# A list scheduler for one in-order TensorE stream: PSUM banks by readiness, small products collected, traced latencies, and an even spread of large products

## The chip, the cores and the metric

The kernel runs on one core of one Trainium2 chip. The metric is the device time of one execution in microseconds (us); of several executions the median is given. TensorE (PE in the profile) multiplies matrices into PSUM, which has eight banks here, each one 128 x 512 fp32 tile. VectorE (DVE) and ScalarE (ACT) do elementwise work, GpSimd (POOL) a few memsets, SyncE (SP) issues the DMAs. Each engine runs its own instructions in the order in which the program issues them.

## The reference

Two layers of a streaming encoder over x of 512 tokens x 1024 channels, all in fp32. Cut to what matters:

```python
for l in range(DEPTH):                                        # DEPTH = 2
    x = x + 0.5 * swiglu_ffn(rmsnorm(x, ffn1_norm[l]), ffn1_w_in[l], ffn1_w_out[l])
    h = rmsnorm(x, mix_norm[l])
    u_rwkv, u_gla, u_xa, u_gate = split_cols(h @ w_in[l], ...)
    y_rwkv, v_first = rwkv7_mixer(u_rwkv, v_first, ...)       # 8 heads of 64, a recurrence over the tokens
    y_gla = gla_mixer(u_gla, ...)                             # 4 heads, chunked linear attention, chunks of 64
    y_xa = memory_attention(u_xa, rmsnorm(mem, mem_norm[l]), xa_w_kv[l])   # 4 heads over 256 memory rows
    gates = jax.nn.sigmoid(u_gate.reshape(b, s, 3, d))
    merged = jnp.einsum('bsjc,jcd,bsjd->bsd', branches, w_branch[l], gates)
    x = x + merged @ w_out[l]
    x = x + 0.5 * swiglu_ffn(rmsnorm(x, ffn2_norm[l]), ffn2_w_in[l], ffn2_w_out[l])
return rmsnorm(x, final_norm)
```

The RWKV recurrence is, per token, `state = state * w + (state . -kk)(kk * a) + v k` and `y = state . r`.

## The kernel before

**Two kinds of products.** A large product is a projection of 128 output channels over all 512 tokens. Its operands are split into a high and a low part (`split` and `weight`: ScalarE writes the high part `whi`, VectorE subtracts it for the low part `wlo`), and for each 128 input channels three passes run (`mm3`: high x high, high x low, low x high), so that a projection of 1024 channels is 24 passes into one PSUM bank, `ps_b`. Small products are those inside RWKV, GLA and the attention heads and in the norms: fp32 matmuls of 64 to 512 columns, each of which runs as two passes, and transposes. They go into the banks `ps_i`, `ps_f`, `ps_c` and `ps_y`.

**PSUM.** Three banks have the tag b (large products), two the tag i (RWKV `gates` and `first`, GLA), and one each f (RWKV `second` and `out`, attention heads, norms, GLA), c (RWKV `inverse`, GLA) and y (RWKV `second`, GLA, and in layer 1 the value product of `rwkv_lora`). A tag is a ring: in the kernel before, the n-th tile of a tag waits, in program order, until the tile that used the same bank last is gone.

**RWKV in units.** Four pairs of heads (`hp`) times two halves of 256 tokens (`hf`) make eight units in a layer. `rwkv_rkv(hp)` multiplies the large products for k and r of a pair into `rk_k` and `rk_r`, each a single buffer. For a unit `rwkv_gates`, `rwkv_first` and `rwkv_inverse` prepare four chunks of 64 tokens (inverse: X, W and Z go round between VectorE and TensorE), `rwkv_second` runs the recurrence over them (per chunk the products S,AR into y, then qs,Z and VU,KBT into f, each waiting for VectorE or ScalarE), its last products are VU,GR, and `rwkv_out` normalises y with a row of small VectorE operations, transposes it (`ps_f<-cst,y`) and multiplies the output gate (`ps_f<-sgl,g`). In `rwkv_fill` the preparation of unit n is recorded ahead of `second` and `out` of unit n-1.

**Fills.** Between the units `rwkv_fill` records independent work with many large products, 18 fills: an attention head (a query projection of 24 passes and its small products), four parts of the GLA branch, a second head, four more parts of the GLA branch, and eight parts of the attention branch. A part of a branch is a gate projection of 24 passes and a branch projection of 12. `share` says how many fills are recorded after each unit; the k and r of the next pair come after them. After the eight units six gates of the RWKV branch (`early`) are recorded. Then the RWKV branch follows: it reads the units' y back, splits it into `yh`, `yl` and multiplies it.

**The planner.** The kernel is recorded first and issued afterwards. Every engine instruction becomes an `Op` with its dependencies; `cost` gives it two prices: `busy`, for which it holds its engine, and `took`, after which its result is there. `lag` adds what lies between two operations: `HOP` (34 ns), and ahead of a TensorE operation 120 ns and a margin, `SLACK`, or 400 ns behind a DMA. `run` simulates all engines; where TensorE is free it takes, in the kernel before, the ready operation with the smallest key `(kind, n)`: small products (kind 0) always ahead of large ones (kind 1), and within a kind by program order n. VectorE and ScalarE take what is due first (`late`, which `urgency` works out from TensorE's order in the pass before). `plan` makes six such passes and keeps the order that ends first by its own clock; `issue` then emits the instructions in that order. Durations of the plan do not reach the chip, only the order does: TensorE waits in its queue for each product's operands. Because all instructions are issued from one place, the profile shows one line, L278, for all of them; they are told apart by their tiles.

Of the kernel before, what the change touches and what calls it, by code (L numbers as in the profile page):

```python
# [11 lines left out]
F32 = mybir.dt.float32  # L12
# [7 lines left out]
P = 128  # L20
T = 512
# [60 lines left out]
class Tile:  # L82
    def __init__(self, pool, shape, dt, name, tag, bufs):
        self.pool, self.shape, self.dt, self.name, self.tag, self.bufs = pool, shape, dt, name, tag, bufs
        self.real, self.users, self.writes, self.reads, self.runs = None, [], [], [], ([], [])
        self.before, self.gone = (), None

# [105 lines left out]
class Pool:  # L193
# [6 lines left out]

    def tile(self, shape, dt, name, tag, bufs=None):
# [30 lines left out]
class Op:  # L232
    def __init__(self, n, engine, what, call, deps):
        self.n, self.engine, self.what, self.call = n, engine, what, call
        self.deps, self.kind, self.pool, self.tile = deps, 1, None, None
        self.busy = self.took = self.start = 0.0
        self.mode = self.table = None

# [9 lines left out]
class Recorder:  # L248
# [3 lines left out]
    def __init__(self, tc):  # L252
        self.tc, self.ops, self.open, self.closed, self.entered, self.kind = tc, [], [], [], [], 0
        for e in self.ENGINES:
            setattr(self, e, Engine(self, e))
# [14 lines left out]
    def add(self, engine, what, a, k):  # L270
# [9 lines left out]
        o = self.op(engine, what, call, ())  # L280
        deps = o.deps
        for v, writes in [(v, False) for v in ins] + [(v, True) for v in outs]:
            t, area = v.tile, v.area()
            assert t.gone is None
            if not t.users or writes:
# [69 lines left out]

    HOP, SLACK = 34, 150

    def lag(self, p, o, slack=True):
# [8 lines left out]
        return self.HOP + s + (120 if o.engine == "tensor" else 0)  # L367

    def run(self, late):

# [5 lines left out]
        events, count, table, last, done = [], 0, None, None, 0  # L376
        order = []
# [22 lines left out]
        while events:  # L400
            t, _, what, o = heapq.heappop(events)
            touched = set()
            while True:
                if what == "ready":
                    if o.engine is None:
                        o.start = t
                        order.append(o)
                        free_up(o)
                    else:
                        heapq.heappush(ready[o.engine], (*key(o), o))  # L410
                        touched.add(o.engine)
                else:
                    touched.add(o)
                if events and events[0][0] <= t:
                    t, _, what, o = heapq.heappop(events)
                else:
                    break
            for e in touched:
                if free[e] > t or not ready[e]:
                    continue  # L420
                if e == "scalar":
                    best = min(ready[e], key=lambda q: q[0] + (2000 if q[-1].table not in (None, table) else 0))
                    ready[e].remove(best)
                    heapq.heapify(ready[e])
                    o = best[-1]
                else:
                    o = heapq.heappop(ready[e])[-1]
                o.start = t
                busy = o.busy
                if e == "tensor":  # L430
                    if last is not None and o.mode != last:
                        busy += 28 if o.mode[1:] == last[1:] else 92
                    last = o.mode
                if e == "scalar" and o.table is not None and o.table != table:
                    table = o.table
                    o.start += 1290
                    busy += 1290
# [24 lines left out]

    def plan(self, passes=6):
        for o in self.ops:
            o.next = []
# [29 lines left out]
class Net:  # L495
# [232 lines left out]
    def rwkv_lora(self):  # L728
        nc = self.nc
        self.wlal = self.lr.tile([P, T], F32, name="wlal", tag="wlal", bufs=1)  # L730
        self.shifted(12, self.wlal)
        nc.scalar.activation(self.wlal[0:64, :], self.wlal[0:64, :], AF.Tanh)
        if self.l > 0:
            ps = self.psy.tile([P, T], F32, name="ps_y", tag="y")
        for q in range(4):
# [12 lines left out]
    def rwkv_rkv(self, hp):  # L748
        nc = self.nc
        wz = self.const.tile([P, 2, P], F32, name="wz", tag="wz", bufs=2)  # L750
        nc.sync.dma_start(out=wz, in_=self.I["wz"][self.l, hp])
# [22 lines left out]
    def rwkv_gates(self, hp, hf, wz, r, k, v):  # L774
        nc, t1 = self.nc, self.t256
        N = 256
        cs = slice(hf * N, (hf + 1) * N)
# [30 lines left out]
    def rwkv_first(self, hp, hf, r, k, v, kk, kh, a, G):  # L808
        nc, rw, t1 = self.nc, self.rw, self.t256
        N = 256  # L810
        ch = lambda a: a.rearrange("p (c t) -> p c t", c=4)
# [97 lines left out]
    def rwkv_inverse(self, Z, AB, AU, W32):  # L909
        nc, rw = self.nc, self.rw  # L910
        flat = lambda q: q.rearrange("p u t -> p (u t)")

# [39 lines left out]
    def rwkv_second(self, hp, hf, E, AR, VU, u0, GR, Z, KBT, bv):  # L952
        nc, rw, t1 = self.nc, self.rw, self.t256
        N = 256
        cs = slice(hf * N, (hf + 1) * N)
        y = t1("y", 2)
        for c in range(4):
# [30 lines left out]

        psy = self.psy.tile([P, T], F32, name="ps_y", tag="y")
        for p in range(2):  # L990
# [10 lines left out]
    def rwkv_out(self, hp, hf, y, bv):  # L1001

        nc, rw, t1 = self.nc, self.rw, self.t256
        N = 256
        cs = slice(hf * N, (hf + 1) * N)
# [90 lines left out]
    def xa_head(self, pool, j, q, kT, vm):  # L1096
        nc = self.nc
        sc = 128.0 ** -0.5
        for hh in range(2):
# [27 lines left out]
    def gla_conv(self, pool, i, out):  # L1127
        nc = self.nc
        ps = self.proj(GQKV + i)
        a = pool.tile([P, T], F32, name="gc", tag="gc", bufs=2)  # L1130
# [6 lines left out]
    def gla_al(self, pool):  # L1137
        nc = self.nc
        w = self.weight(self.I["w_al"][self.l], KD, 16)
        ps = self.big()  # L1140
# [6 lines left out]
    def gla_decay(self, pool, hp, al):  # L1147
        nc = self.nc
        ps = self.small()
        nc.tensor.matmul(ps, self.aup[:, hp * P:(hp + 1) * P], al, start=True, stop=True)  # L1150
# [13 lines left out]
    def gla_pair(self, pool, hp, al, yh, yl, between):  # L1164
        nc = self.nc
        t = lambda name, bufs=1: pool.tile([P, T], F32, name=name, tag=name, bufs=bufs)
        E, F = self.gla_decay(pool, hp, al)
        between()
        q, k = t("gq"), t("gk", 2)
        self.gla_conv(pool, hp, q)  # L1170
# [62 lines left out]
        for j in range(2):  # L1233
            h = 2 * hp + j
            ps = self.psy.tile([P, T], F32, name="ps_y", tag="y")
            for p in range(4):
# [210 lines left out]
```

## Time and profile before

| what | value |
|---|---|
| median of 3 runs | 2769.85 us (2769.09 to 2770.24) |
| the profiled execution: its time, its span | 2769.8 us, 2768.0 us |
| mean granted TensorE clock | 0.995 |
| TensorE busy | 2731.8 us (99%), 13280 matmul passes |
| VectorE, ScalarE busy | 1570.7 us (57%), 1164.9 us (42%) |
| DMA | 258.04 MB, 93 GB/s on average |

In time order, layer 0's RWKV units run from about 560 to 940 us, layer 1's from about 1925 to 2315. How to read the rows: a row of the timeline has start, duration, engine, line, operation, tile written<-tiles read, shapes, number of instructions, and in brackets the idle time of the engine ahead of it and what ended it. Matmuls are pipelined and their ends are modelled, so the step from one start to the next says more than a duration. A row of a stretch has the stretch, its length, then for TensorE, its weight loads, VectorE, ScalarE (and POOL) busy time and count, and at the end the granted clock, the share of the DMA engines and GB/s. A row for one tile has the operation, count, durations in ns (least, median, greatest) and the first and the last start.

### The profile page before, as it was taken

The page shows a single profiled execution, that of the slowest core. Times are in us where ns is not written, and L with a number is a line of the kernel's source. Part 1 is how long each engine was busy: PE and PEld are TensorE (multiplying, and loading weights), DVE is VectorE, ACT ScalarE, POOL GpSimd, SP SyncE. Part 2 cuts the span into 40 slices and gives each one's busy share as a digit, 9 for nine tenths or more (in the row PEclk, how much of TensorE's full clock was granted, in tenths as well). Part 3 has the DMA queues.
Part 4 walks back from the last instruction along what each step waited for, and adds up shares of the span by engine and source line. Part 5 has one row for each costly group of instructions (what it writes and reads, how often), then busy time and mean ns, then how long its engine had stood idle before and what let it go on. Part 6 is the DMA issues. An engine that isn't in the chain of part 4 may idle for free. (4 is left out here: it accounts for less than half of the span.)

```text
span 2768.0 us, 35481 instructions
## 1 busy us (share of the span) xinstructions
PE 2731.8 (99%) x13280; PEld 2225.2 (80%) x13280; DVE 1570.7 (57%) x3056; ACT 1164.9 (42%) x2150; POOL 19.8 (1%) x102
## 2 busy tenths in 40 slices
PE   8999999999999999999999999999999999999998
PEld 7888888887787788888888888877777877888886
DVE  6434456677668654444454343666775786543444
ACT  6323356455445343233343232664553453432332
POOL 0000000000000000000000000000000000000000
PEclk9999999999999999999999999999999999999999
DMA  5232332211222232222332323322212112322322
GB/s 194 90 101 99 102 135 77 100 59 67 85 71 68 69 115 99 89 102 94 104 107 89 102 99 114 132 83 77 67 63 91 67 58 78 117 95 89 106 90 86
DMA packets 91723, 258.04 MB, mean 93 GB/s; under 512 B 10464, under 2 KB 24832, under 8 KB 91552
## 3 DMA queue, kind: packets, MB, share of 16 engines
q1 hardware_dynamic: 91552, 255.79, 27.5%
q8 instruction: 104, 1.70, 0.3%
q14 instruction: 67, 0.55, 0.1%
HBM read 243.69 MB, written 12.06 MB: 92 GB/s over the span
## 5 line engine op out<-in xcount | busy, mean ns | idle before, releaser
L278 ACT ACTIVATE whi<-wraw 128x512 fp32r<-128x512 f32 (+1 forms) x874 | 544.0, 623 | 1191.6 <-PE ps_b L278 1155.9
L278 PE MATMUL ps_b<-xhi,whi 128*128 128x512 f32 x2288 | 905.5, 396 | 8.2 <-ACT whi L278 8.2
L278 DVE TENSOR_TENSOR wlo<-wraw,whi 128x512 fp32r<-128x512 f32 (+1 forms) x874 | 590.9, 677 | 564.3 <-ACT whi L278 549.1
L278 PE MATMUL ps_b<-xhi,wlo 128*128 128x512 f32 x2288 | 904.4, 395 | 0.0
L278 PE MATMUL ps_b<-xlo,whi 128*128 128x512 f32 x2288 | 904.3, 395 | 0.0
L278 PEld LDWEIGHTS ps_b<-xhi,whi 128*128 128x128 f32 x2288 | 429.2, 188 | 97.4 <-ACT whi L278 8.6
L278 PEld LDWEIGHTS ps_b<-xlo,whi 128*128 128x128 f32 x2288 | 429.0, 187 | 90.6 <-issue 3.5
L278 PEld LDWEIGHTS ps_b<-xhi,wlo 128*128 128x128 f32 x2288 | 429.0, 188 | 89.3 <-issue 2.5
L278 PE MATMUL ps_b<-mhi,whi 128*128 128x512 f32 x704 | 277.4, 394 | 0.0
L278 PE MATMUL ps_b<-mhi,wlo 128*128 128x512 f32 x704 | 276.0, 392 | 0.0
L278 PE MATMUL ps_b<-mlo,whi 128*128 128x512 f32 x704 | 273.2, 388 | 0.0
L278 PEld LDWEIGHTS ps_b<-mhi,wlo 128*128 128x128 f32 x704 | 132.2, 188 | 31.0
L278 PEld LDWEIGHTS ps_b<-mlo,whi 128*128 128x128 f32 x704 | 132.1, 188 | 29.6
L278 PEld LDWEIGHTS ps_b<-mhi,whi 128*128 128x128 f32 x704 | 132.4, 188 | 26.3
L278 DVE TENSOR_TENSOR fm<-ps_b,ft 128x512 f32<-128x512 f32 x88 | 60.9, 692 | 124.5 <-PE ps_b L278 124.4
L278 DVE TENSOR_TENSOR ft<-ps_b,rs 128x512 f32<-128x512 f32 x88 | 60.9, 692 | 121.5 <-PE ps_b L278 121.2
L278 PE MATMUL ps_b<-yh,whi 128*128 128x512 f32 (+1 forms) x256 | 97.2, 383 | 5.0 <-ACT yh L278 5.0
L278 ACT ACT_TABLE_LOAD x73 | 93.7, 1283 | 11.0 <-DMA par<-in_par_dram 5.6
L278 PE MATMUL ps_b<-yl,whi 128*128 128x512 f32 (+1 forms) x256 | 97.8, 382 | 0.0
L278 PE MATMUL ps_b<-yh,wlo 128*128 128x512 f32 (+1 forms) x256 | 95.8, 377 | 0.0
L278 DVE SCALAR_TENSOR_TENSOR x<-ps_b,x 128x512 f32<-128x512 f32 x64 | 44.3, 692 | 62.2 <-PE ps_b L278 62.2
L278 DVE TENSOR_TENSOR ft<-ft,rs 128x512 f32<-128x512 f32 x88 | 60.9, 693 | 14.1 <-ACT ft L278 6.3
(260 smaller groups left out, 2746.6 us busy)
## 6 DMA issues: line engine op xcount, KB each, us to landing
wraw<-in_ffn_in_dram SPq DMA_DIRECT2D x176, 512.0 KB, 3.5
wraw<-in_w_main_dram SPq DMA_DIRECT2D x108, 512.0 KB, 3.5
wraw<-in_ffn_out_dram SPq DMA_DIRECT2D x64, 512.0 KB, 3.5
wraw<-in_ffn_out_dram SPq DMA_DIRECT2D x64, 192.0 KB, 2.3
wraw<-in_w_branch_dram SPq DMA_DIRECT2D x48, 256.0 KB, 2.6
wraw<-in_w_out_dram SPq DMA_DIRECT2D x16, 512.0 KB, 3.5
xd<-x SPq DMA_DIRECT2D x16, 256.0 KB, 2.2
wraw<-in_w_k_dram SPq DMA_DIRECT2D x8, 512.0 KB, 3.6
```

The costliest lines, as they stand in the source:

```text
L278: return getattr(getattr(self.tc.nc, engine), what)(*(f(v) for v in a), **{n: f(v) for n, v in k.items()})
```

## The change

It edits the planner and the order of recording; no operation's shape, operand or number changes.

1. `cost`: the time until a TensorE result can be read is raised, for transposes from 60 to 275 ns, for large passes from n/2.4 - 36 to n/2.4 + 177, for small fp32 products from `2 passes - 45` (up to 128 columns; + 55, + 100 above) to one pass + two column times + 168. The margin `SLACK` ahead of TensorE goes from 150 to 60 ns, the price of a turn between large and small from 28 to 45, that of an activation table from 1290 to 1400.
2. `choose` replaces "small ahead of large": behind a small product, ready small products go on, those of the same shape of array first; behind a large product small ones are taken only when ready ones of 400 ns are together or one has been ready for 600 ns; otherwise the next large one goes.
3. Tiles of the tags f, c and y are made with `free=True`. They no longer wait for the tile ahead of them in program order across all parts, only for their own part's (`nc.part`: lora, rkv, gates, first, inverse, second, out, xa, gla). In `run` the first operation of such a tile takes a bank if one is free (`slot`), or is held until one is given back.
4. `rwkv_fill`: `share` goes from five fills after a unit (15 after the first three units, the rest after the fourth) to two after each of the eight, the last two behind all units.

```diff
 class Pool:
+    def tile(self, shape, dt, name, tag, bufs=None, free=False):
         t = Tile(self, shape, dt, name, tag, bufs)
+        t.free = free
         ring = self.tags.setdefault(tag, [])
-        t.before = [self.rec.gone(ring[-bufs])] if len(ring) >= bufs else list(self.before)
+        t.before = [self.rec.gone(ring[-bufs])] if len(ring) >= bufs and not free else list(self.before)
+        if free:
+            own = self.tags.setdefault((tag, self.rec.part), [])
+            if len(own) >= bufs:
+                t.before.append(self.rec.gone(own[-bufs]))
+            own.append(t)
...
     def cost(self, o, ins, outs, a, k):
             if o.what == "transpose":
-                o.busy, o.took = 109, 60
+                o.busy, o.took = 109, 275
             elif ins[0].dt == F32R:
                 o.busy = n / 2.4 + 13.7
-                o.took = o.busy - 50
+                o.took = n / 2.4 + 177
             else:
                 o.busy = 2 * max(108 if wide else 58, 2 * n / 2.4 + 2.7)
-                o.took = o.busy + (-45 if n <= 128 else 55 if n <= 256 else 100)
+                o.took = o.busy / 2 + 2 * n / 2.4 + 168
...
-    HOP, SLACK = 34, 150
+    HOP, SLACK = 34, 60
...
+    HOLD = 600
+    def choose(self, ready, last, est, t):
+        small = [q for q in ready if q[0] == 0]
+        big = min((q for q in ready if q[0]), default=None)
+        if not small:
+            return big
+        same = [q for q in small if q[-1].mode == last]
+        if same:
+            return min(same)
+        if big is None or (last is not None and not last[0]):
+            return min(small)
+        first = min(small)
+        if sum(q[-1].busy for q in small) >= 400 or t - min(est[q[-1]] for q in small) >= self.HOLD:
+            return first
+        return big
...
     def run(self, late):
+        def slot(o):
+            t = o.takes
+            if t is None:
+                return True
+            k = t.pool, t.tag
+            if used.get(k, 0) < t.bufs:
+                used[k] = used.get(k, 0) + 1
+                return True
+            held.setdefault(k, []).append(o)
+            return False
...
+                while ready[e]:
+                    if e == "tensor":
+                        o = self.choose(ready[e], last, est, t)
+                        ...
+                    if slot(o):
+                        break
...
-                        busy += 28 if o.mode[1:] == last[1:] else 92
+                        busy += 45 if o.mode[1:] == last[1:] else 92
...
     def small(self, tag="f"):
-        return self.pss.tile([P, T], F32, name="ps_" + tag, tag=tag, bufs=2 if tag == "i" else 1)
+        return self.pss.tile([P, T], F32, name="ps_" + tag, tag=tag, bufs=2 if tag == "i" else 1, free=tag != "i")
...
-                psq = self.psy.tile([P, T], F32, name="ps_y", tag="y")
+                psq = self.psy.tile([P, T], F32, name="ps_y", tag="y", free=True)
...
     def rwkv_fill(self, rkv, fill):
-        share = [0, 5, 5, 5, 5, 5, 5, 4, 4]
+        share = [0, 2, 2, 2, 2, 2, 2, 2, 2]
```

More of the change, by code (lines that the diff above doesn't have):

```diff
@@ L85, in __init__ @@
         self.real, self.users, self.writes, self.reads, self.runs = None, [], [], [], ([], [])
-        self.before, self.gone = (), None
+        self.before, self.gone, self.free = (), None, False
     def make(self):
@@ L199, in __init__ @@
             ctx.callback(self.close)
-    def tile(self, shape, dt, name, tag, bufs=None):
+    def tile(self, shape, dt, name, tag, bufs=None, free=False):
         bufs = bufs or self.bufs
         t = Tile(self, shape, dt, name, tag, bufs)
+        t.free = free
         ring = self.tags.setdefault(tag, [])
-        t.before = [self.rec.gone(ring[-bufs])] if len(ring) >= bufs else list(self.before)
+        t.before = [self.rec.gone(ring[-bufs])] if len(ring) >= bufs and not free else list(self.before)
[4 more added lines that the diff above has]
+            own.append(t)
         ring.append(t)
@@ L236, in __init__ @@
         self.busy = self.took = self.start = 0.0
-        self.mode = self.table = None
+        self.mode = self.table = self.takes = None
 class Engine:
@@ L253, in __init__ @@
         self.tc, self.ops, self.open, self.closed, self.entered, self.kind = tc, [], [], [], [], 0
+        self.part = None
         for e in self.ENGINES:
@@ L283, in add @@
             t, area = v.tile, v.area()
+            if t.free and not t.users:
+                o.takes = t
             assert t.gone is None
@@ L376, in run @@
         events, count, table, last, done = [], 0, None, None, 0
-        order = []
+        order, used, held = [], {}, {}
         def key(o):
             return (o.kind, o.n) if o.engine == "tensor" else (late[o], o.n)
+        def slot(o):
[8 more added lines that the diff above has]
+            return False
         def put(t, what, o):
@@ L408, in run @@
                         free_up(o)
+                        if o.tile is not None and o.tile.free:
+                            k = o.tile.pool, o.tile.tag
+                            used[k] -= 1
+                            for q in held.pop(k, ()):
+                                put(t + self.lag(o, q), "ready", q)
                     else:
@@ L418, in run @@
             for e in touched:
-                if free[e] > t or not ready[e]:
+                if free[e] > t:
                     continue
[L421 to L425, printed above, removed]
+                while ready[e]:
+                    if e == "tensor":
+                        o = self.choose(ready[e], last, est, t)
+                        ready[e].remove(o)
+                        heapq.heapify(ready[e])
+                        o = o[-1]
+                    elif e == "scalar":
+                        best = min(ready[e], key=lambda q: q[0] + (2000 if q[-1].table not in (None, table) else 0))
+                        ready[e].remove(best)
+                        heapq.heapify(ready[e])
+                        o = best[-1]
+                    else:
+                        o = heapq.heappop(ready[e])[-1]
+                    if slot(o):
+                        break
                 else:
-                    o = heapq.heappop(ready[e])[-1]
+                    continue
                 o.start = t
@@ L435, in run @@
                     table = o.table
-                    o.start += 1290
-                    busy += 1290
+                    o.start += 1400
+                    busy += 1400
                 free[e] = t + busy
@@ L463, in plan @@
     def plan(self, passes=6):
+        for t in {o.takes: None for o in self.ops if o.takes is not None}:
+            self.gone(t)
         for o in self.ops:
@@ L729, in rwkv_lora @@
         nc = self.nc
+        nc.part = "lora"
         self.wlal = self.lr.tile([P, T], F32, name="wlal", tag="wlal", bufs=1)
@@ L733, in rwkv_lora @@
         if self.l > 0:
-            ps = self.psy.tile([P, T], F32, name="ps_y", tag="y")
+            ps = self.psy.tile([P, T], F32, name="ps_y", tag="y", free=True)
         for q in range(4):
@@ L749, in rwkv_rkv @@
         nc = self.nc
+        nc.part = "rkv"
         wz = self.const.tile([P, 2, P], F32, name="wz", tag="wz", bufs=2)
@@ L775, in rwkv_gates @@
         nc, t1 = self.nc, self.t256
+        nc.part = "gates"
         N = 256
@@ L809, in rwkv_first @@
         nc, rw, t1 = self.nc, self.rw, self.t256
+        nc.part = "first"
         N = 256
@@ L910, in rwkv_inverse @@
         nc, rw = self.nc, self.rw
+        nc.part = "inverse"
         flat = lambda q: q.rearrange("p u t -> p (u t)")
@@ L953, in rwkv_second @@
         nc, rw, t1 = self.nc, self.rw, self.t256
+        nc.part = "second"
         N = 256
@@ L986, in rwkv_second @@
                                                        ALU.mult, ALU.add)
-        psy = self.psy.tile([P, T], F32, name="ps_y", tag="y")
+        psy = self.psy.tile([P, T], F32, name="ps_y", tag="y", free=True)
         for p in range(2):
@@ L1003, in rwkv_out @@
         nc, rw, t1 = self.nc, self.rw, self.t256
+        nc.part = "out"
         N = 256
@@ L1097, in xa_head @@
         nc = self.nc
+        nc.part = "xa"
         sc = 128.0 ** -0.5
@@ L1128, in gla_conv @@
         nc = self.nc
+        nc.part = "gla"
         ps = self.proj(GQKV + i)
@@ L1138, in gla_al @@
         nc = self.nc
+        nc.part = "gla"
         w = self.weight(self.I["w_al"][self.l], KD, 16)
@@ L1148, in gla_decay @@
         nc = self.nc
+        nc.part = "gla"
         ps = self.small()
@@ L1165, in gla_pair @@
         nc = self.nc
+        nc.part = "gla"
         t = lambda name, bufs=1: pool.tile([P, T], F32, name=name, tag=name, bufs=bufs)
@@ L1168, in gla_pair @@
         between()
+        nc.part = "gla"
         q, k = t("gq"), t("gk", 2)
@@ L1234, in gla_pair @@
             h = 2 * hp + j
-            ps = self.psy.tile([P, T], F32, name="ps_y", tag="y")
+            ps = self.psy.tile([P, T], F32, name="ps_y", tag="y", free=True)
             for p in range(4):
```

## The prediction

> **What bounds the kernel now.** I read the page's totals first, then TensorE's work by stretches, then its instructions in order of time, and last its waits.
>
> ```profile
> span 2768.0 us, 35481 instructions
> PE 2731.8 (99%) x13280; PEld 2225.2 (80%) x13280; DVE 1570.7 (57%) x3056; ACT 1164.9 (42%) x2150; POOL 19.8 (1%) x102
> ```
> TensorE is never idle for long, VectorE and ScalarE are at about a half: the end is set by TensorE's in-order stream. But "99% busy" is a modelled end, so I go by start-to-start steps. Timeline of TensorE, layer 0:
>
> ```profile
> 719.70 0.39 PE L278 MATMUL ps_b<-yh,whi 128*128 128x512 f32 x1
> 719.93 0.39 PE L278 MATMUL ps_b<-yl,whi 128*128 128x512 f32 x1
> 720.15 0.39 PE L278 MATMUL ps_b<-yh,wlo 128*128 128x512 f32 x1
> ...
> 700.74 1.00 PE L278 MATMUL ps_c<-X,abd 128*128 128x64 f32 x8
> 701.58 0.44 PE L278 MATMUL ps_y<-S,AR 128*128 128x128 f32 x2
> 701.78 0.48 PE L278 MATMUL ps_b<-xhi,whi 128*128 128x512 f32 x1
> 702.09 0.40 PE L278 MATMUL ps_b<-xlo,whi 128*128 128x512 f32 x1
> ```
> A large product (into ps_b, 512 wide) costs 0.227 us, start to start. The ten small passes and one large from 700.74 to 702.09 take 1.35 us, so a small pass takes (1.35 - 0.227) / 10 = 0.112 us, and here turning from large to small and back costs nothing. Now the count of everything, by stretch and tile (columns: stretch, TensorE busy and instructions, then weight loads, VectorE, ScalarE):
>
> ```profile
> 0.00:2768.00 2768.00, 2422.99 (x10224) 1888.37 (x10224) 269.81 (x388) 71.41 (x114) 1.00 0.28 93
> ...
> L278 PE MATMUL ps_b<-yl,whi 128*128 128x256 f32 x64 | 18.1, 283 | 0.0
> ...
> PE ps_b L278 <- ACT whi L278: 8.2, 1, 8.2
> ...
> 2757.35 2.08 PE L278 MATMUL ps_f<-cst,rt 128*128 128x128 f32 x8 [0.57 <-DVE rt L278]
> ```
> Of 10,224 passes into ps_b, 192 are 256 wide (three groups of 64; 0.120 us each), 10,032 are 512 wide: 2277.3 + 23.0 = 2300 us. The other 13,280 - 10,224 = 3,056 are small: about 2,360 at 0.112, 384 of half the columns at 0.058, 256 of 256 elements at 0.216, 56 of 512 at 0.431: 366 us. The first weights come at 8.2 us, the last product's second pass starts 9.0 before the end. 2768.0 - 2300 - 366 - 17 = 85 us: that is all that reordering can win; products, bytes and passes stay the same.
>
> Where do the 85 lie? First, at the end of the RWKV part of each layer:
>
> ```profile
> 936.52 0.39 PE L278 MATMUL ps_b<-yh,wlo 128*128 128x512 f32 x1
> 938.11 0.41 PE L278 MATMUL ps_f<-cst,y 128*128 128x128 f32 x2 [1.21 <-DVE y L278]
> 938.36 0.60 PE L278 MATMUL ps_f<-sgl,g 128*128 128x256 f32 x2
> 941.61 1.65 PE L278 MATMUL ps_b<-yh,whi 128*128 128x512 f32 x3 [2.65 <-ACT yh L278]
> 943.05 0.63 PE L278 MATMUL ps_b<-yl,whi 128*128 128x512 f32 x1
> ...
> 947.24 0.40 PE L278 MATMUL ps_b<-yh,whi 128*128 128x512 f32 x1
> ...
> 943.00:947.20 4.20, 4.20 (x11) 3.27 (x10) 2.73 (x5) 1.89 (x3) 0.00 (x0) 0.51 0.00 0
> ...
> 2312.64 0.39 PE L278 MATMUL ps_b<-yh,wlo 128*128 128x512 f32 x1
> 2314.24 0.41 PE L278 MATMUL ps_f<-cst,y 128*128 128x128 f32 x2 [1.20 <-DVE y L278]
> 2317.38 1.65 PE L278 MATMUL ps_b<-yh,whi 128*128 128x512 f32 x3 [2.30 <-ACT yh L278]
> 2322.92 0.39 PE L278 MATMUL ps_b<-yh,whi 128*128 128x512 f32 x1
> ```
> No large product is left; TensorE waits for the last unit's y, then for its halves yh, and afterwards runs at a granted clock of 0.51, 0.43 us a product. From 936.52 to 947.24 stand 14 large and four small passes (3.18 + 0.66 us), so 10.72 - 3.84 = 6.9 us are lost; from 2312.64 to 2322.92 in the same way 10.28 - 3.84 = 6.4. **Tails: 13.3 us.** They come from the order of the fills:
>
> ```profile
> L278 DVE SCALAR_TENSOR_TENSOR rk_k<-ps_b,omu,rk_k x1: 753/753/753, 785.7 to 785.7; 128x512 f32<-128x512 f32 x1
> L278 PE MATMUL ps_y<-VU,GR x8: 275/275/284, 736.9 to 737.7; 128*128 128x128 f32 x8
> L278 PE MATMUL ps_y<-VU,GR x8: 275/275/328, 837.0 to 838.4; 128*128 128x128 f32 x8
> L278 PE MATMUL ps_y<-VU,GR x8: 275/275/275, 860.4 to 861.2; 128*128 128x128 f32 x8
> L278 DVE SCALAR_TENSOR_TENSOR rk_k<-ps_b,omu,rk_k x4: 743/750/753, 566.1 to 853.9; 128x512 f32<-128x512 f32 x4
> 610.00:938.00 328.00, 322.99 (x1821) 260.18 (x1820) 230.59 (x626) 151.60 (x370) 5.27 (x25) 1.00 0.20 67
> 610.00:740.00 130.00, 86.66 (x307) 54.41 (x307) 6.32 (x9) 5.51 (x9) 1.00 0.20 65
> 740.00:796.00 56.00, 54.14 (x236) 43.72 (x235) 4.85 (x7) 4.29 (x7) 1.00 0.30 97
> 796.00:938.00 142.00, 89.27 (x306) 53.66 (x304) 3.55 (x5) 6.71 (x11) 1.00 0.17 56
> ```
> (The row of 610 to 938 counts all of TensorE, the other stretches only what touches ps_b.) The fourth RWKV unit ends at 737, the fifth at 837, the sixth at 860: the fifth's k is written only at 785.7, because that large product stands behind 15 of the 18 fills in program order. From 740 to 796 TensorE does large products alone (236 x 0.227 = 54 us), and from 796 the chain has too few of them.
>
> Second, the rest, 85 - 13 = 72 us. Reading all starts of the timeline, small passes stand in 390 stretches between large ones; 204 cost under 0.1 us beyond their passes (4 us together), 184 more than that outside the tails, 53 us together; some 9 us is drift of 0.227 to 0.232 between large ones. The dear ones are waits:
>
> ```profile
> PE ps_f L278 <- DVE y L278: 6.5, 11, 1.2
> 662.02 0.30 PE L278 MATMUL ps_i<-VU,MA 128*64 128x64 f32 x2 [0.41 <-DVE GR L278]
> 746.98 0.41 PE L278 MATMUL ps_f<-cst,y 128*128 128x128 f32 x2 [1.07 <-DVE y L278]
> 711.68 0.44 PE L278 MATMUL ps_f<-qs,Z 128*128 128x128 f32 x2
> 712.16 0.45 ACT L278 ACTIVATE VU<-ps_f 64x64 f32<-64x64 f32 x2 [0.73 <-PE ps_f L278]
> ```
> The order was planned with operands that come sooner than they do, and TensorE stands in front of them while large work is ready behind.
>
> **The change, part by part.**
> 1. *Result times.* For a 128-wide small product the old plan starts the reader 218.7 - 45 + 34 = 208 ns after the product; the trace has 480 (711.68 to 712.16). The new one says 109 + 107 + 168 + 34 = 418. For a transpose it goes from 94 to 309. In return the margin before TensorE falls from 150 to 60: per round trip the plan grows by 210 - 90 = 120 ns. This issues nothing; it moves small products later behind large ones. 184 late stretches x 0.12 = 22 us won; bounds 0 (they are late for other reasons, as y behind a weight split on VectorE) and 53.
> 2. *Collecting.* After a large product, small ones are issued only when 400 ns of them are ready or one has waited 600. Batches of four or more (0.9 us) go at once; single ones (qs,Z; VU,KBT; S,AR; two transposes: 0.22 us) wait for company. Turning costs about nothing here, so fewer turnings win nothing in themselves, but the hold is more margin; against it, what is taken right behind another small one has 90 ns less margin than now. I take 0, between -10 and +10. Price on the chain: some 13 single steps per unit x 0.6 = at most 8 us.
> 3. *Free banks* (f, c, y). Who is ready first takes the bank, instead of program order. No instruction is added; a memory-attention head may hold f while the RWKV state waits. RWKV tiles of one part keep their order. 0, between -3 and +3.
> 4. *Switch costs and table load* in the plan's prices: no instruction, 0.
> 5. *Share 2 instead of 5.* The products for k and r of the third, fifth and seventh unit now stand behind 2, 6 and 10 fills instead of 5, 15 and 18. From 610 to 938 small passes are 1821 - (307 + 236 + 306) = 972, at 366 / 3056 = 0.12 us 117 us, 14.6 a unit. Per pair of units TensorE then has 29 us of small passes, 10.9 of k and r (48 x 0.227) and four fills of 36 x 0.227 = 8.2, 33: 73 us, 36 a unit. The fifth and sixth unit follow each other at 23 us, plus at most 8 of hold: the chain keeps up. Behind the last k and r stand eight fills and six early gates, 65 + 33 = 98 us of large work (a fill has a product of 24 passes and one of 12, a gate one of 24), and 36 of small (two and a half units): 134 us of cover, where the chain from the last k (853.9) to its last small product (938.4) took 85. So the tails go with their clock loss: -13.3. What is late next is again TensorE itself: the merge finds y ready.
>
> Sum against the profiled execution: 2768.0 - 13.3 - 22 + 0 + 0 = 2732.7, and 2.0 I add, an estimate, for new waits where small work is mixed into the 54 us that were large alone (a third of the 6.5 that y is waited for now). That execution took 2769.8 with 1.8 around its span; the median is 2769.85. So 2734.7 + 1.8, rounded **2736 us**. Under 0.2% (5.5 us) a measurement of this kernel can't tell from no change.
>
> [...]
>
> **Rivals.**
> A, slower: k and r of the next pair are multiplied before the last pair has read its own, and stand in two of the three large banks; no large product can follow.
>
> ```profile
> L278 DVE SCALAR_TENSOR_TENSOR t<-t,rk_k x2: 415/418/420, 574.3 to 590.7; 128x256 f32<-128x256 f32 x2
> ```
> k is written at 566 and read last at 591, 25 us. Two fills alone are 13.6 us; without small work between them TensorE would stand 11 us, six times: 68 - 35 = 33 us slower, 2803. It decides where the large work ahead of k falls under the chain's 25 us. Against it: 29 us of small passes lie between, too.
> B, the tails go and the small stretches stay as dear: 2768 - 13.3 + 1.8 = 2757.
> C, the hold lengthens the chain by 8 us x 8 = 64, more than the 50 us of spare cover: tails stay, 2768 - 22 + 1.8 = 2748.
> D, nothing: what the new order wins at the tails it pays in stretches: 2770.
> E, nearly all late stretches go: 2768 - 13.3 - 45 + 1.8 = 2712.
>
> **How the numbers follow.** Forecast 0.56 (2722 to 2750), E 0.08, B 0.15, C 0.04, D 0.07, A 0.10. Faster 0.83, same 0.07, slower 0.10. The range 2709 to 2764 takes in the forecast, E's middle, B and C.
>
> **What would show it.** In the profile after: full clock and no wait of ps_b for yh over 1 us behind the RWKV part; the units' k spaced evenly, the pause of 100 us between the fourth and fifth unit gone; fewer than 390 small stretches; the wait of ps_f for y under 6.5 us. Wrong would be waits of ps_b for rk_k or rk_r, or as many stretches over 0.1 us as now.

## The result, and the profile after

The changed kernel takes 2738.07 us (median of 4, 2737.55 to 2738.72) against 2769.68 before: ratio 0.9886, interval 0.9869 to 0.9903. The forecast was 2736. The sum came out; how it is shared among the parts did not, as the experiments show.

Totals and TensorE's longest waits in the changed kernel (all instructions now stand in line L286):

```profile
span 2736.4 us, 35439 instructions
PE 2705.0 (99%) x13280; PEld 2228.5 (81%) x13280; DVE 1568.6 (57%) x3056; ACT 1163.0 (43%) x2148; POOL 19.8 (1%) x102
...
PE ps_b L286 <- ACT whi L286: 8.1, 1, 8.1
PE ps_f L286 <- DVE sqa L286: 2.3, 1, 2.3
PE ps_f L286 <- DVE y L286: 2.3, 4, 0.7
```
The passes are the same 13,280; the span is 31.6 us shorter. Of the waits shown before, the two for yh (5.0 us) are gone and those for y went from 6.5 to 2.3. The end of layer 0's RWKV part, once the place of the first tail, now reads:

```profile
881.61 0.39 PE L286 MATMUL ps_b<-xhi,whi 128*128 128x512 f32 x1
881.84 0.38 PE L286 MATMUL ps_f<-cst,y 128*128 128x128 f32 x2
882.06 0.60 PE L286 MATMUL ps_f<-sgl,g 128*128 128x256 f32 x2
882.30 0.58 PE L286 MATMUL ps_b<-xlo,whi 128*128 128x512 f32 x1
882.72 0.39 PE L286 MATMUL ps_b<-xhi,wlo 128*128 128x512 f32 x1
...
880.00:960.00 80.00, 80.00 (x355) 66.19 (x354) 41.28 (x67) 30.15 (x52) 0.00 (x0) 1.00 0.33 112
...
L286 DVE SCALAR_TENSOR_TENSOR rk_k<-ps_b,omu,rk_k x4: 746/748/751, 559.6 to 780.4; 128x512 f32<-128x512 f32 x4
```
The last unit's y is multiplied in the middle of large work, at 882 instead of 938, and TensorE stays at full clock (1.00). The last pair's k is written at 780 instead of 854: the spread brought it forward, as planned.

To compare kernels I read all starts of TensorE and subtract each pass's own step, as in the prediction. "Pauses" are stretches that lose over 2.5 us; the rest is split into stretches that use the whole array throughout and those that turn its shape (with products on fewer than 128 rows or columns of the array). The slow clock behind a pause is not in these columns. Where exactly a stretch is cut moves a column by up to 3 us; the counts and the sum of the three columns hardly move.

| kernel | median us | small stretches | pauses | rest, no turn | rest, with turns |
|---|---|---|---|---|---|
| before | 2769.7 | 390 | 2, 8.8 us | 33.9 us | 22.8 us |
| share_only | 2762.2 | 361 | 0 | 41.3 | 21.7 |
| before_margin | 2763.9 | 399 | 2, 22.9 | 16.5 | 19.7 |
| after | 2738.1 | 313 | 0 | 20.3 | 17.7 |
| share_back | 2771.6 | 321 | 2, 38.3 | 14.6 | 13.4 |
| times_back | 2741.1 | 311 | 0 | 22.0 | 19.0 |
| collect_back | 2751.3 | 356 | 0 | 31.5 | 20.0 |
| margin_instead | 2730.6 | 357 | 0 | 10.3 | 19.3 |
| hold1200 | 2741.1 | 283 | 2, 5.8 | 18.1 | 15.5 |
| banks_back | 2753.8 | 322 | 3, 21.3 | 12.1 | 17.6 |
| cy_free | 2754.0 | 322 | 3, 20.4 | 12.0 | 18.1 |
| f_free | 2738.2 | 313 | 0 | 20.6 | 17.6 |
| slack200 | 2728.6 | 315 | 0 | 11.4 | 15.1 |
| slack360 | 2726.8 | 313 | 0 | 14.6 | 11.6 |

From before to after: 8.8 us of pauses and some 4 of slow clock (0.51 from 943.00 to 947.20, 0.54 from 2319 to 2323) behind them, and (33.9 + 22.8) - (20.3 + 17.7) = 18.7 in the small stretches: together about 32.

### The profile page after: what moved, and what is told of

Read it like the earlier page. It is cut to its first block, busy times and chain, and to the rows that moved or that the text cites. A ratio compares the mean times of both kernels' runs of the same rounds, so it can differ in the third digit from the quotient of the medians.

```text
span 2736.4 us, 35439 instructions
## 1 busy us (share of the span) xinstructions
PE 2705.0 (99%) x13280; PEld 2228.5 (81%) x13280; DVE 1568.6 (57%) x3056; ACT 1163.0 (43%) x2148; POOL 19.8 (1%) x102
## 4 chain that ended last, share of the span: by engine, by line
PE 91%; DVE 6%; ACT 1%; issue 1%; DMA 1%; DVEq 0%; SPq 0%; ACTq 0%
PE ps_b L286 80%; PE ps_i L286 3%; PE ps_c L286 3%; PE ps_f L286 3%; PE ps_y L286 2%; DVE wlo L286 1%; DVE knrm L286 1%; DVE y L286 0%; DVE S L286 0%; DMA yd<-sg 0%; DVE Z L286 0%; DVE x L286 0%; ACT whi L286 0%; DVE t L286 0%; DVE A L286 0%
## 5 line engine op out<-in xcount | busy, mean ns | idle before, releaser
L286 ACT ACTIVATE whi<-wraw 128x512 fp32r<-128x512 f32 (+1 forms) x874 | 543.8, 623 | 1166.0 <-PE ps_b L286 1117.3
L286 DVE TENSOR_TENSOR wlo<-wraw,whi 128x512 fp32r<-128x512 f32 (+1 forms) x874 | 591.0, 677 | 578.9 <-ACT whi L286 565.6
L286 PE MATMUL ps_b<-xhi,whi 128*128 128x512 f32 (+1 forms) x2288 | 902.0, 394 | 8.3 <-ACT whi L286 8.1
L286 PE MATMUL ps_b<-xlo,whi 128*128 128x512 f32 (+1 forms) x2288 | 901.9, 394 | 0.1
L286 PE MATMUL ps_b<-xhi,wlo 128*128 128x512 f32 (+1 forms) x2288 | 901.5, 394 | 0.0
L286 PEld LDWEIGHTS ps_b<-xhi,whi 128*128 128x128 f32 (+1 forms) x2288 | 428.9, 187 | 98.8 <-ACT whi L286 8.1
L286 PEld LDWEIGHTS ps_b<-xlo,whi 128*128 128x128 f32 (+1 forms) x2288 | 428.8, 187 | 91.5 <-issue 3.2
L286 PEld LDWEIGHTS ps_b<-xhi,wlo 128*128 128x128 f32 (+1 forms) x2288 | 428.8, 187 | 90.8 <-issue 3.4
L286 PE MATMUL ps_b<-mhi,whi 128*128 128x512 f32 x704 | 277.4, 394 | 0.0
L286 PE MATMUL ps_b<-mhi,wlo 128*128 128x512 f32 x704 | 276.0, 392 | 0.0
L286 PE MATMUL ps_b<-mlo,whi 128*128 128x512 f32 x704 | 273.2, 388 | 0.0
L286 PEld LDWEIGHTS ps_b<-mhi,wlo 128*128 128x128 f32 x704 | 132.2, 188 | 31.0
L286 PEld LDWEIGHTS ps_b<-mlo,whi 128*128 128x128 f32 x704 | 132.1, 188 | 29.6
L286 PEld LDWEIGHTS ps_b<-mhi,whi 128*128 128x128 f32 x704 | 132.3, 188 | 26.3
L286 DVE TENSOR_TENSOR fm<-ps_b,ft 128x512 f32<-128x512 f32 x88 | 60.9, 692 | 124.7 <-PE ps_b L286 124.6
L286 DVE TENSOR_TENSOR ft<-ps_b,rs 128x512 f32<-128x512 f32 x88 | 60.9, 692 | 120.2 <-PE ps_b L286 120.0
L286 PE MATMUL ps_b<-yh,whi 128*128 128x512 f32 (+1 forms) x256 | 95.7, 374 | 0.0
L286 PE MATMUL ps_b<-yh,wlo 128*128 128x512 f32 (+1 forms) x256 | 95.3, 372 | 0.0
L286 PE MATMUL ps_b<-yl,whi 128*128 128x512 f32 (+1 forms) x256 | 95.0, 371 | 0.0
L286 DVE SCALAR_TENSOR_TENSOR x<-ps_b,x 128x512 f32<-128x512 f32 x64 | 44.3, 692 | 62.4 <-PE ps_b L286 62.4
L286 DVE TENSOR_TENSOR ft<-ft,rs 128x512 f32<-128x512 f32 x88 | 60.9, 693 | 11.7 <-ACT ft L286 3.6
```

What stands on the lines that cost most here:

```text
L286: return getattr(getattr(self.tc.nc, engine), what)(*(f(v) for v in a), **{n: f(v) for n, v in k.items()})
```

## The experiments

Each ratio is to the kernel before on the same chip.

**share_only**: the kernel before with one line of the change.

```diff
-        share = [0, 5, 5, 5, 5, 5, 5, 4, 4]
+        share = [0, 2, 2, 2, 2, 2, 2, 2, 2]
```

> The kernel before with one part of the change: two fills after each unit instead of five. Theory (tails come from the order of the fills, small stretches from the plan's result times): both tails go, 13 us, and the small stretches stay as dear: about 2756, no slow clock behind the RWKV units, about 390 small stretches. Rival (the tails went because of the accurate plan or the banks, not the spread): no change, 2770, both waits of ps_b for yh of over 2 us still there.

2762.24 us, ratio 0.9971 (0.9961 to 0.9982): 7.7 us faster, where 13 were expected. The tails did go; no wait for yh is left:

```profile
PE ps_b L278 <- ACT whi L278: 8.0, 1, 8.0
PE ps_f L278 <- DVE sqa L278: 2.3, 1, 2.3
PE ps_f L278 <- DVE qs L278: 2.1, 3, 1.1
PE ps_f L278 <- DVE y L278: 1.7, 5, 0.5
```
But the small stretches became dearer by (41.3 + 21.7) - (33.9 + 22.8) = 6 us, all of it in those without a turn. The likely reason is that TensorE now meets small products whose operands are late where large products alone stood before; no run shows that by itself.

**share_back**: the changed kernel with the old share (the diff above turned round).

> The changed kernel with the old share (five fills after a unit), all else as changed. Theory: the two tails are back with their slow clock, +13 us: about 2751. Rival (the accurate plan alone covers the chain's end): within 3 us of 2738.

2771.59, ratio 1.0005 (0.9996 to 1.0014): without the spread the other three parts win nothing at all. The pauses of the tails are 38.3 us where the kernel before has 8.8, and the slow clock comes on top. TensorE in layer 0's tail:

```profile
919.91 0.38 PE L286 MATMUL ps_f<-VU,KBT 128*128 128x128 f32 x2
921.54 0.41 PE L286 MATMUL ps_f<-cst,y 128*128 128x128 f32 x2 [1.25 <-DVE S L286]
...
924.05 0.76 PE L286 MATMUL ps_f<-qs,Z 128*128 128x128 f32 x2 [1.44 <-DVE y L286]
925.40 0.80 PE L286 MATMUL ps_f<-VU,KBT 128*128 128x128 f32 x2 [0.60 <-ACT VU L286]
...
940.32 0.66 PE L286 MATMUL ps_f<-cst,y 128*128 128x128 f32 x2 [5.78 <-DVE y L286]
...
922.00:941.00 19.00, 8.52 (x29) 6.29 (x28) 7.33 (x27) 3.11 (x11) 0.00 (x0) 0.55 0.00 0
```
The large work is used up at 920, most of the last unit's recurrence is still to come, and it runs alone: 29 passes in 19 us, at a granted clock of 0.55. The small stretches of this kernel meanwhile cost 28 us, half of those before. A plan that holds small products back spares TensorE waits but lengthens the chain, and with the old share the chain ends last (before_margin, below, shows the same with the margin alone).

**times_back**: the changed kernel with the old prices.

```diff
-                o.busy, o.took = 109, 275
+                o.busy, o.took = 109, 60
-                o.took = n / 2.4 + 177
+                o.took = o.busy - 50
-                o.took = o.busy / 2 + 2 * n / 2.4 + 168
+                o.took = o.busy + (-45 if n <= 128 else 55 if n <= 256 else 100)
-    HOP, SLACK = 34, 60
+    HOP, SLACK = 34, 150
...
```

> The changed kernel with the old prices in the plan (result times, margin of 150 ns, turns, table load); spread, banks and collecting as changed. Theory of the prediction: late stretches come back, about 0.12 us each in some 100 to 180 of them, +12 to +22 us: 2750 to 2760. Rival (the hold alone gives the margin that the small products lacked): within 4 us of 2738.

2741.05, ratio 0.9898 (0.9883 to 0.9913): 3 us, the rival's number, and the interval overlaps that of the change (0.9869 to 0.9903). Once the hold is there, the traced result times with their smaller margin are worth little. What they are worth without the hold is another question; see the next section.

**collect_back**: the changed kernel without collecting.

```diff
-                        o = self.choose(ready[e], last, est, t)
+                        o = min(ready[e])
```

> The changed kernel with the old choice, small products always ahead of large ones; result times, banks and spread as changed. Theory of the prediction: collecting is worth nothing by itself: 2738 within 4 us, with more small stretches (about 390) that are as cheap as now. Rival (the hold is what keeps TensorE from standing in front of late operands): late stretches come back, 2748 to 2758.

2751.31, ratio 0.9931 (0.9919 to 0.9944): 13 us slower than the change, again the rival's number. A late stretch in it, TensorE with ScalarE:

```profile
689.37 0.49 PE L286 MATMUL ps_f<-qs,Z 128*128 128x128 f32 x2
...
690.63 0.40 PE L286 MATMUL ps_b<-xhi,whi 128*128 128x512 f32 x1
691.35 0.49 PE L286 MATMUL ps_f<-VU,KBT 128*128 128x128 f32 x2 [0.33 <-ACT VU L286]
...
690.22 0.61 ACT L286 ACTIVATE whi<-wraw 128x512 fp32r<-128x512 f32 x1
690.85 0.45 ACT L286 ACTIVATE VU<-ps_f 64x64 f32<-64x64 f32 x2
```
VU ends at 691.30 and TensorE starts at 691.35. VU reads the product qs,Z of 689.37, but it could not start before the weight split in front of it ended at 690.83, 1.46 us after that product's start; in the prediction's row such a reader started after 0.48. Here TensorE's own result was not late, another engine's queue was; a true price for the product does not help against that, a margin does. How common this is can be sorted roughly by the trace. In this run 94 stretches without a turn lose over 0.1 us. In 44 of them the operand that came last was made by an operation that had started right behind an unrelated one on its own engine, in 7 by one that a TensorE result had released; 11 are steps of a chain on one engine, and for 32 the trace names no cause. In the kernel before, the same sorting gives 126 such stretches, 54 of the first kind and 22 behind a TensorE result.

**margin_instead** asks whether collecting wins by its delay or by having fewer stretches: collect_back with a larger margin.

```diff
-    HOP, SLACK = 34, 60
+    HOP, SLACK = 34, 360
```

> The changed kernel with the old choice (small products always ahead of large ones) and a margin of 360 ns ahead of TensorE in the plan in place of 60. Theory M (collecting wins by its delay: a held product's operand has come when TensorE reaches it): the margin does the same, 2738 to 2743, the stretches without a turn of shape have a median under 15 ns beyond their passes. Theory T (collecting wins by fewer stretches and turns of the array's shape): the stretches stay as many, 2748 to 2752.

2730.58, ratio 0.9857 (0.9844 to 0.9871): 20.7 us faster than collect_back and 7.5 faster than the change, with as many stretches as collect_back (357 and 356). Those without a turn lose 8 ns in the median, 10 us together instead of 31.5. That is theory M's mechanism, with a time even below its range: a delay alone, without fewer stretches, brings all that collecting brought and more.

**hold1200**: the changed kernel with `HOLD = 1200`.

> The changed kernel with a hold of 1200 ns in place of 600. Theory T: fewer stretches and turns, 2730 to 2736. Theory M: held products were already late enough, 2738 within 3 us. The rival of the prediction's C: the chain gets longer and the RWKV part's end shows waits, over 2745.

2741.08, ratio 0.9895 (0.9882 to 0.9909). The stretches did get fewer (283), and nothing was won. Two pauses came in, 2.8 us in the first norm (at 27.6) and 2.9 in layer 1's RWKV part (at 2125.3). It misses the first theory's number and is at the edge of the second's.

**banks_back**: the changed kernel without free banks.

```diff
-        t.free = free
+        t.free = free = False
```

> The changed kernel with all tags in program order again (no free banks); result times, collecting and spread as changed. Theory of the prediction: worth nothing, 2738 within 3 us. Rival (what is left of the gain when the other three parts are taken together, 32 - 8 - 13 - 3 = 8 us, is the banks'): 2744 to 2750.

2753.82, ratio 0.994 (0.9926 to 0.9953): 16 us slower than the change, more than either expectation had. Three pauses of 6.4 to 7.7 us are in its RWKV parts. Two more runs ask which bank it is.

**f_free** and **cy_free**: free banks for the tag f alone, and for c and y alone.

```diff
-        t.free = free
+        t.free = free = free and tag == 'f'        # cy_free: tag != 'f'
```

> The changed kernel with free banks for the tag f alone; c and y in program order. Theory F (the wait for the bank f, which the normalisation of the unit before or an attention head holds in program order, lets the recurrence fall behind the k and r products, so that the large banks stand full): all of the 16 us are the bank f's: 2738 within 4 us, no stretch over 5 us. Rival (the bank y or c): near 2754, the three stretches of 6 to 8 us still there.

> The changed kernel with free banks for the tags c and y; f in program order. Theory F: 2754 within 4 us, stretches of 6 to 8 us in front of the recurrence. Rival: 2738 within 4 us.

f_free 2738.18, ratio 0.9887 (0.9874 to 0.9901); cy_free 2753.98, 0.9944 (0.9931 to 0.9956). All of it is the bank f.

Timeline of cy_free, layer 1, first what uses the bank f after the first unit, then the pause; last its clock by stretch:

```profile
1993.11 0.61 PE L286 MATMUL ps_y<-VU,GR 128*128 128x128 f32 x4
...
2002.94 0.38 PE L286 MATMUL ps_f<-cst,y 128*128 128x128 f32 x2
...
2005.48 1.10 PE L286 MATMUL ps_f<-kT,xq 128*128 128x256 f32 x4
...
2022.26 1.02 PE L286 MATMUL ps_f<-pt,vm 128*128 128x256 f32 x4
2023.96 0.44 PE L286 MATMUL ps_f<-qs,Z 128*128 128x128 f32 x2
...
2054.55 0.48 PE L286 MATMUL ps_b<-yh,wlo 128*128 128x512 f32 x1
2055.77 0.49 PE L286 MATMUL ps_f<-VU,KBT 128*128 128x128 f32 x2 [0.74 <-ACT VU L286]
2056.26 0.47 ACT L286 ACTIVATE sg<-ps_i,half 128x256 f32<-128x256 f32 x1 [0.54 <-DMA yd<-sg]
2057.37 0.49 PE L286 MATMUL ps_y<-S,AR 128*128 128x128 f32 x2 [1.11 <-DVE S L286]
2058.94 0.42 DVE L286 TENSOR_TENSOR AR<-rk_r,E 128x256 f32<-128x256 f32 x1
2059.95 3.09 PE L286 MATMUL ps_i<-AR,KB 64*128 64x128 f32 x16 [1.05 <-DVE KB L286]
2061.04 0.75 DVE L286 SCALAR_TENSOR_TENSOR rk_r<-ps_b,omu,rk_r 128x512 f32<-128x512 f32 x1 [0.94 <-ACT VU L286]
2064.10 0.80 PE L286 MATMUL ps_b<-xhi,whi 128*128 128x512 f32 x1
...
2055.00:2060.00 5.00, 1.55 (x8) 0.95 (x7) 3.81 (x11) 3.01 (x9) 0.10 (x1) 0.94 0.38 127
2060.00:2065.00 5.00, 5.00 (x22) 4.34 (x23) 3.49 (x10) 3.69 (x11) 0.00 (x0) 0.50 0.01 2
```
The first unit ends at 1993. In program order the bank f then belongs to its normalisation (cst,y at 2003) and to a whole attention head (kT,xq to pt,vm, up to 2023): the second unit's qs,Z comes only at 2024, 31 us behind the first unit's end. So the second unit's own output is sent late, and the fourth unit's gates wait for that transfer, since they write the buffer sg that the output is sent from (2056.26, released by yd<-sg). So r is read for the last time only at 2058.94, and until then the next pair's r stands in a large bank (written out at 2061.04). From 2054.6 to 2064.1 not one large product runs. That is rival A of the prediction, with another cause: not too few fills ahead of k, but a chain held up by a bank. In f_free the recurrence goes first and the normalisation follows it:

```profile
1990.03 0.61 PE L286 MATMUL ps_y<-VU,GR 128*128 128x128 f32 x4
...
1995.32 0.38 PE L286 MATMUL ps_f<-qs,Z 128*128 128x128 f32 x2
1997.17 0.38 PE L286 MATMUL ps_f<-VU,KBT 128*128 128x128 f32 x2
1999.25 0.40 PE L286 MATMUL ps_f<-cst,y 128*128 128x128 f32 x2
```
The second unit's qs,Z stands 5.3 us behind the first unit's end.

**before_margin**: the kernel before with one number changed.

```diff
-    HOP, SLACK = 34, 150
+    HOP, SLACK = 34, 360
```

> The kernel before with one number changed: the plan's margin ahead of TensorE 360 ns in place of 150. Theory M (small stretches are dear because operands come later than planned): stretches without a turn of shape fall to under 15 ns in the median, about 25 us; the tails stay and grow by the longer chain, 13 to 25 us: 2745 to 2760. Rival (the margin helps only with the spread and the free banks): the chain's delay eats it all, 2765 to 2780.

2763.9, ratio 0.998 (0.9971 to 0.9989), between the two expectations. The small stretches fell as foreseen, from 33.9 + 22.8 to 16.5 + 19.7, 20 us; the tails took 14 back, 8.8 to 22.9:

```profile
PE ps_f L278 <- DVE y L278: 12.9, 6, 5.8
...
PE ps_b L278 <- ACT yh L278: 4.6, 2, 2.3
```
The wait for y went from 6.5 to 12.9 us, the longest single one from 1.2 to 5.8.

**slack200** and **slack360**: the changed kernel with `SLACK` 200 and 360 in place of 60.

> The changed kernel with a margin of 200 ns in place of 60 in the plan, collecting kept. Theory M: what is taken right behind another small product has too little margin, so late stretches get fewer: 2728 to 2735. Theory T: nothing to win by margin, 2738 within 3 us, or slower by a longer chain.

> The changed kernel with a margin of 360 ns in place of 60, collecting kept: a version to beat both. Theory M: beyond 200 ns there are few late operands left, 2723 to 2729; if the chain gets too long for the spread, waits of the large banks come and it is slower than 2729.

2728.55, ratio 0.985 (0.9836 to 0.9863), and 2726.82, ratio 0.9845 (0.9832 to 0.9859). Both are in theory M's range and beat the change; slack360, 11 us under it, is the lowest time here, though its interval overlaps that of slack200. What margin and hold together leave is 26 us in small stretches, 12 to 15 of them with turns. Beside margin_instead, which has the same margin without collecting, slack360 loses 7.7 us less in stretches with turns and 4.3 more in those without: with a margin in place, collecting seems to win by turns after all. But the intervals of the two kernels overlap, so the 3.8 us between their times are not clear of noise.

## Why the prediction was right, and where its steps were wrong

By place, the prediction held. The bound was read rightly: passes and their steps stay, and 85 us of loss were all there was to win. The tails were to give 13.3 us and gave about 13; the small stretches were to give 22 less 2 and gave 18.7. The signs it named came too: stretches that lose over 0.1 us fell from 184 to about 86, and the wait for y from 6.5 to 2.3. By part of the change it held for the spread alone. That the 22 us, worked out for the result times alone, came so near to what three parts brought together is luck.

*Step 5, the spread*, held. The tails and their slow clock are gone, the k of the last pair comes 74 us earlier. Alone the spread wins 7.7 us instead of 13.3, since the mixing it brings costs 6; the 2.0 put in for that was too little. With the other parts in place its removal costs 33.5: the price of a fill order depends on how long the chain is.

*Step 1, result times*, was mis-sized: 22 us in the sum, 3 when taken out beside the hold. Without the hold they bring more: from share_only to collect_back, on the same chip, come the new prices (with their smaller margin) and the free banks, and the time falls from 2762.24 to 2751.31, 11 us for the two together. The prediction took the late operands for the plan's short time from a product to its reader (208 ns, where the trace had 480). collect_back plans 418 ns and still loses 31.5 us in stretches without a turn; of its late ones about half are late behind other work on VectorE or ScalarE, as far as the trace tells, and only 7 of 94 behind a TensorE result.

*Step 2, collecting*, was put at 0 between -10 and +10 and is worth 13. The prediction named the hold as "more margin" and then priced it at nothing. margin_instead shows that a margin alone gives as much and more. Of what collecting took off the stretches, 11.2 us were in those without a turn (31.5 to 20.3) and 2.3 in those with turns.

*Step 3, free banks*, was put at 0 within 3 and is worth 16. The step asked who might hold f while the state waits after the change, and not who holds it in program order: the normalisation of the unit that has just ended, and a head. What the free banks, or the result times, would be worth in the kernel before alone was not run.

So 22 + 0 + 0 stood for 3, 13 and 16, which don't add up either: taken out one at a time, the four parts cost 33.5, 3, 13 and 16 us, 65 together, of a gain of 32. Added in one order they do add up: the spread 7.7, result times and banks 11, collecting 13. They hang together: delays win only where the spread leaves the chain room, and the spread wins only where the chain keeps its pace.

Rival A had the right mechanism at 0.10 and came true in banks_back and cy_free; the changed kernel escapes it by part 3. In the kernel before, TensorE went on at full clock behind the pause of 1.07 us ahead of 746.98 (1.00 from 745 to 752). In cy_free four pauses of 0.55 to 1.11 us came one after the other from 2055 to 2060, none from 2054 to 2064 is shown longer than 1.11, and the clock was 0.50 from 2060 to 2068. What TensorE waited for there were operands of the recurrence while the large banks stood full. That the row of pauses brought the clock down was not tested by a run of its own. In the changed kernel no such place is left, and its mean clock is 0.998 against 0.995. Rival C, a chain longer than its cover, is what share_back shows, though which of hold, prices and banks lengthens it there was not separated; with the new share the cover of 50 us was enough.

That "turning from large to small and back costs nothing" held in these two kernels for products that use the whole array (at most 0.05 us a stretch in the median) and was wrong for most of the others (0.32 to 0.33); see the last section.

## What to carry to other kernels

An engine that runs a planned order in sequence pays for each operand that comes later than planned, whatever the reason for the delay. A plain margin ahead of it, 300 ns more, won 20 us here with one number, where exact prices, 120 ns more per round trip with their smaller margin, won 3 beside the hold and at most 11 without it. The two are not equal doses, but a margin also covers delays that a price for TensorE's result does not. Such a margin is paid by the dependent chain, so first give the chain independent work to its very end, and look which ring buffer ties its next step to the last step's tidying up or to a fill. Parts that are worth 33, 16, 13 and 3 us when removed can win 32 together: test them by leaving out as well as by adding.

## What the runs showed of the hardware that was not expected

Stretches with products on part of the array's rows or columns lost more than the others. TensorE in the changed kernel, first in one of them that lost 0.40 us:

```profile
527.30 0.40 PE L286 MATMUL ps_b<-xhi,whi 128*128 128x512 f32 x1
527.63 0.48 PE L286 MATMUL ps_i<-qz,kg 64*128 64x128 f32 x2
...
528.40 0.38 PE L286 MATMUL ps_i<-qr,kr 64*128 64x128 f32 x2
528.71 0.50 PE L286 MATMUL ps_b<-xlo,whi 128*128 128x512 f32 x1
529.05 0.39 PE L286 MATMUL ps_b<-xhi,wlo 128*128 128x512 f32 x1
...
527.63 0.29 PEld L286 LDWEIGHTS ps_i<-qz,kg 64*128 64x128 f32 x2 [0.37 <-issue]
529.05 0.19 PEld L286 LDWEIGHTS ps_b<-xhi,whi 128*128 128x128 f32 x1
...
647.44 1.71 PE L286 MATMUL ps_i<-AR,KB 64*128 64x128 f32 x16
649.08 0.49 PE L286 MATMUL ps_f<-VU,KBT 128*128 128x128 f32 x2
```
From 527.30 to 529.05 are two large passes and eight small ones, 0.454 + 0.896 us of own steps in 1.75: 0.40 us is lost with no wait for an operand shown. In this trace the weight load of the first small product starts with its own matmul at 527.63, 0.33 us after the large one at 527.30, while the load at 529.05, for the large product that comes at 529.28, starts with the large matmul ahead of it. The stretches with turns of shape lose 0.32 us in the median before and 0.33 after, those with none at most 0.05 and 0.01. That the turn itself is the cause was not tested by a run of its own; some of these stretches wait for operands as well.

Another stretch with a turn took less than its own steps. The 16 passes of AR,KB, eight on one half of the rows and eight on the other, take 1.64 us up to the next start (647.44 to 649.08), where 16 x 0.112 would be 1.79. In the trace three of them start 4 to 6 ns behind the pass ahead; eleven start 105 to 112 ns behind it.

In cy_free the granted clock fell without a long idle time: with only 1.55 us of work in the 5 from 2055 to 2060 and no idle time shown above 1.11, it was 0.94 in these 5 and 0.50 in the next 5. The pause had ended at 2064.10, and from 2065 to 2068, with TensorE busy throughout, the clock was still 0.50.
